# Low parts of split weights in the scan stage: an adding DMA onto a negated copy, in place of a GpSimd subtraction

## The chip, the cores and the metric

The kernel runs on one core of a Trainium2 chip. The metric is the time of one execution on the device in microseconds (us), the median of several runs.

## What is computed

One layer of a hybrid backbone: 512 latent tokens of width 1024, with 256 context tokens whose scan states start the latent scans. The part that the change touches is the input projection and the three branches that read it:

```
h    = modulated_norm(x, g_norm1, sh1, sc1)
proj = h @ w_in                      # 1024 x 7712, cut into z, xBC, dt, pool, gmlp, gates
xbc  = silu(dwconv(proj[xBC]))       # 5 taps
y    = ssd_scan(...)  both directions, 128-token chunks, states from the context
y_pool = box means of proj[pool];  y_gmlp = u * (ws @ layernorm(v))
x    = x + g1 * ((gates * branches) @ w_o)
x    = x + g2 * moe(...)             # top-1 group, top-2 experts, 16 experts
out  = rmsnorm(x)
```

All in float32.

## The kernel before

Each weight matrix is multiplied in three products of float32r (a rounded float32 that TensorE takes at full speed): rounded weights by rounded activations, rounded weights by the activations' remainder, and the weights' remainder by rounded activations. So every weight unit, a tile of 128 x 1024 float32 (512 KB), is loaded from HBM into a ring of four buffers (`raw`), and `split` makes two tiles of it: `hi`, which ScalarE copies and rounds (L87), and `lo = raw - hi` (L89), from rings of three buffers each. Which engine does the subtraction is set by `lo_eng`. It is VectorE (`V`) at the start and from the SSD norm on, and GpSimd (`G`) between: from the first pair of `x` channels in the scan loop to the end of the gMLP branch.

```
        S.activation(hi[:, :n], raw[:, :n], AF.Copy)
        with tc.issue_after(after.ins) if after else nullcontext():
            eng.tensor_tensor(lo[:, :n], raw[:, :n], hi[:, :n].bitcast(FT), op=OP.subtract)
```

That stretch, called the scan stage here, runs from about 60 to 415 us. In it 34 units go through GpSimd. The loop over four head groups does, for each group, four `xbc_tile` calls (one unit each: projection, then the convolution as one ScalarE and four VectorE operations `cv` on L968 and L970, a silu, transposes on TensorE), `ssd_decay` (the DMA `agb<-agd` on L1112, then ScalarE and VectorE operations on L1119 to L1133), in every second group a `z_block` (four units, a `tm_block`), and `ssd_group` (states on L1075 to L1085, outputs on L1094 to L1104). After the loop come the pooling mixer (VectorE sums on L1260 to L1280) and the gMLP branch (L1215 to L1237), with 12 units more.

The order of the instructions on each engine is made by a scheduler when the program is built. At run time each engine follows its own list in order and waits on semaphores. TensorE (PE) takes a unit's `hi` in the first products and its `lo` in the product of L105 (in `xbc_tile` and `cm_block`) or L1145 (in `tm_block`). SyncE (SP) issues the loads of `raw` and `agb` in one in-order queue, and a load into a `raw` buffer waits until the subtraction that last read the buffer is done. GpSimd (POOL) also issues some small DMAs, and late in the kernel the scatter `eod<-eo` of L445, an adding DMA of 512 KB to HBM.

Of the kernel before, what the change touches and what calls it, by code (L numbers as in the profile page):

```python
# [11 lines left out]
AF = mybir.ActivationFunctionType  # L12
OP = mybir.AluOpType
# [30 lines left out]
def backbone_kernel(ctx: ExitStack, tc: tile.TileContext, x, c, ctxt, c_ctx, w_mod, b_mod, g_norm1,  # L44
# [4 lines left out]
    V, S, G, T = nc.vector, nc.scalar, nc.gpsimd, nc.tensor  # L49
# [31 lines left out]
    def split(raw, n, after=None):  # L81
        nsplit[0] += 1
        eng = G if lo_eng[0] is None and nsplit[0] % 1000 == 3 else lo_eng[0] or V
        hp_, lp_ = more_hl if more_hl and nsplit[0] % 4 == 0 else (hip, lop)
        hi = hp_.tile([128, 1024], FR, tag="hi", name="hi")
        lo = lp_.tile([128, 1024], FR, tag="lo", name="lo")
        S.activation(hi[:, :n], raw[:, :n], AF.Copy)  # L87
        with tc.issue_after(after.ins) if after else nullcontext():
            eng.tensor_tensor(lo[:, :n], raw[:, :n], hi[:, :n].bitcast(FT), op=OP.subtract)  # L89
        return hi, lo  # L90

    def unit(ap, k, n):
        raw = rawp.tile([128, 1024], FT, tag="raw", name="raw")
        nc.sync.dma_start(raw[:, :k * n].rearrange("p (k n) -> p k n", k=k), ap)
        hi, lo = split(raw, k * n)
        return (hi[:, :k * n].rearrange("p (k n) -> p k n", k=k),
                lo[:, :k * n].rearrange("p (k n) -> p k n", k=k))
# [31 lines left out]
    def late_rows(stack, rd):  # L129

        ap_ = stack.enter_context(pool("lrow"))
        oner = ap_.tile([128, 4], FR)
        V.tensor_copy(oner, ones[:, 0:4])

        def block(b):
            a = ap_.tile([128, D], FT, tag="lacc", name="lacc")
            G.memset(a, 0.0)
            nc.sync.dma_start(a[0:1], dap(b_mod, (2 + b) * D, [[D, 1], [1, D]]))
            for k in range(KD):
                raw = rawp.tile([128, 1024], FT, tag="raw", name="raw")  # L140
                nc.sync.dma_start(raw, dap(w_mod, k * 128 * 6144 + (2 + b) * D, [[6144, 128], [1, D]]))
                V.scalar_tensor_tensor(a, raw, sc[:, k:k + 1], a, op0=OP.mult, op1=OP.add)  # L142
            hi, lo = split(a, D)
            r = ap_.tile([1, D], FT, name="lr", tag="lr")
            if b == 2:
                gn = rawp.tile([128, 1024], FT, tag="raw", name="gn2")[0:1]
                nc.sync.dma_start(gn, dap(g_norm2, 0, [[D, 1], [1, D]]))
            for h in range(2):
                cs = slice(h * 512, (h + 1) * 512)
                pr = ptmp([4, 512])  # L150
                T.matmul(pr, lhsT=oner, rhs=hi[:, cs], start=True, stop=False)
                T.matmul(pr, lhsT=oner, rhs=lo[:, cs], start=False, stop=True)
                if b == 2:
                    V.scalar_tensor_tensor(r[:, cs], pr[0:1], 1.0, gn[:, cs], op0=OP.add, op1=OP.mult)
                else:
                    S.activation(r[:, cs], pr[0:1], AF.Copy)
            nc.sync.dma_start(rd[b:b + 1], r)
        return block
# [189 lines left out]
    def moe(q):  # L348
# [29 lines left out]
        def munit(e, k, out_w, widx):  # L378
            rows = w2rows if out_w else w1rows
            if widx is None:  # L380
                n = nraw[0] % 31
                nraw[0] += 1
                raw = ring[n]
                if isinstance(raw, tuple):
                    raw = raw[0].tile([128, 1024], FT, tag=raw[1], name=raw[1])
                r0 = e * (DE if out_w else D) + k * 128
                nc.sync.dma_start(raw, rows[r0:r0 + 128])
            else:
                raw = rawp.tile([128, 1024], FT, tag="raw", name="raw")
                c0 = k + (KD if out_w else 0)  # L390
                G.indirect_dma_start(out=raw, out_offset=None, in_=rows,
                                     in_offset=bass.IndirectOffsetOnAxis(ap=widx[:, c0:c0 + 1], axis=0))
            return split(raw, 1024, chain[0] if widx is None and nraw[0] <= 4 else None)
# [992 lines left out]
```

## Time and profile before

| | us |
|---|---|
| median of 3 runs (1037.62 to 1039.67) | 1037.87 |
| the profiled execution's own time | 1038.74 |
| its span in the trace | 1036.9 |
| busy in the span: PE | 946.9 (91%) |
| busy: VectorE (DVE) | 820.9 (79%) |
| busy: ScalarE (ACT) | 596.9 (58%) |
| busy: GpSimd (POOL) | 189.7 (18%), of it 91.1 in the 34 subtractions of L89 |

The time of an execution is the span and 1.84 us around it. Busy shares are means over stages with different limits: PE is the fullest engine, and yet a stretch can be set by a chain of small steps on other engines. The chain of work that ended last is 64% PE and 22% DVE over the whole span.

### The profile page before, as it was taken

What the parts mean: (1) busy time and instruction counts of PE and PEld (TensorE: products, weight loads), DVE (VectorE), ACT (ScalarE), POOL (GpSimd) and SP (SyncE); (2) the same over time, 40 slices, a digit from 0 to 9 for tenths busy, and PEclk for the clock granted to TensorE, in tenths of its full rate; (3) what the DMA queues carried; (4) which work ended last, traced back from release to release, by engine and by line L of the source; (5) the groups of instructions that cost most, each with busy time, mean ns of one, the idle gap of its engine ahead of it and who ended that gap; (6) DMA issues with size and microseconds to landing.
All of it is one profiled execution on the core that took longest, in us unless ns stands there. A gap on an engine that the chain in (4) does not pass through costs nothing.

```text
span 1036.9 us, 13348 instructions
## 1 busy us (share of the span) xinstructions
PE 946.9 (91%) x4598; PEld 769.4 (74%) x4598; DVE 820.9 (79%) x1221; ACT 596.9 (58%) x884; POOL 189.7 (18%) x144
## 2 busy tenths in 40 slices
PE   3897989998898979999999999978999999999964
PEld 0486778886786857888888888867888888888842
DVE  6878976997878996677486434579999999999897
ACT  5665846667556333622332432445788888888843
POOL 2024313114222340000000010331111111111140
PEclk9998999999999989999999999988999999999987
DMA  8832361314223222276576558678999999999322
GB/s 271 280 91 60 119 201 41 116 47 143 61 61 86 64 65 71 82 244 215 172 217 210 162 166 288 257 245 318 326 355 362 361 375 372 375 361 364 107 73 82
DMA packets 100898, 203.92 MB, mean 197 GB/s; under 512 B 9998, under 2 KB 55290, under 8 KB 100827
## 3 DMA queue, kind: packets, MB, share of 16 engines
q1 hardware_dynamic: 95474, 194.19, 54.5%
q0 software_dynamic: 5136, 8.78, 3.6%
q8 instruction: 37, 0.61, 0.2%
q14 instruction: 35, 0.28, 0.1%
q10 hardware_dynamic: 216, 0.07, 0.0%
HBM read 197.25 MB, written 13.71 MB: 203 GB/s over the span
## 4 chain that ended last, share of the span: by engine, by line
PE 64%; DVE 22%; ACT 5%; DMA 4%; issue 3%; ACTq 0%; POOL 0%; SPq 0%; DVEq 0%; POOLq 0%
PE pacc L104 18%; PE pacc L103 18%; PE pacc L105 18%; DVE cv L970 5%; DVE lo L89 2%; PE ptmp L400 1%; DMA wraw<-in_w_mod_dram 1%; DVE w L1132 1%; DMA agb<-agd 1%; PE ptmp L1094 1%; PE ptmp L1096 1%; DVE agb L1126 1%; PE ptmp L423 1%; DVE r L1274 1%; DVE y L1103 1%
## 5 line engine op out<-in xcount | busy, mean ns | idle before, releaser
L87 ACT ACTIVATE hi<-raw 128x1024 fp32r<-128x1024 f32 (+1 forms) x199 | 209.0, 1057 | 168.0 <-PE pacc L104 75.9
L89 DVE TENSOR_TENSOR lo<-raw,hi 128x1024 fp32r<-128x1024 f32 (+1 forms) x165 | 203.6, 1254 | 58.8 <-ACT hi L87 51.7
L103 PE MATMUL pacc<-hTh,hi 128*128 128x512 f32 (+1 forms) x392 | 156.7, 401 | 4.9 <-ACT ytok L1168 3.5
L104 PE MATMUL pacc<-hTl,hi 128*128 128x512 f32 (+1 forms) x392 | 158.0, 403 | 0.0
L105 PE MATMUL pacc<-hTh,lo 128*128 128x512 f32 (+1 forms) x392 | 156.6, 400 | 0.0
L104 PE MATMUL pacc<-lo,xhl 128*128 128x512 f32 x384 | 151.5, 395 | 4.2 <-DVE lo L89 3.9
L103 PE MATMUL pacc<-hi,xhl 128*128 128x512 f32 x384 | 153.1, 402 | 0.0
L105 PE MATMUL pacc<-hi,xhl 128*128 128x512 f32 x384 | 150.5, 393 | 0.0
L89 POOL TENSOR_TENSOR lo<-raw,hi 128x1024 fp32r<-128x1024 f32 x34 | 91.1, 2684 | 197.6 <-ACT hi L87 187.8
L103 PEld LDWEIGHTS pacc<-hTh,hi 128*128 128x128 f32 (+1 forms) x392 | 74.0, 189 | 21.5 <-ACT ytok L1168 3.9
L104 PEld LDWEIGHTS pacc<-lo,xhl 128*128 128x128 f32 x384 | 72.9, 190 | 20.4 <-DVE lo L89 6.1
L970 DVE SCALAR_TENSOR_TENSOR cv<-xr,pcol,cv 128x770 f32<-128x770 f32 (+1 forms) x64 | 70.9, 1108 | 20.9 <-ACT cv L968 20.2
L105 PEld LDWEIGHTS pacc<-hTh,lo 128*128 128x128 f32 (+1 forms) x392 | 73.9, 189 | 16.2 <-issue 1.0
L104 PEld LDWEIGHTS pacc<-hTl,hi 128*128 128x128 f32 (+1 forms) x392 | 74.0, 189 | 16.0 <-issue 1.1
L105 PEld LDWEIGHTS pacc<-hi,xhl 128*128 128x128 f32 x384 | 72.5, 189 | 15.5
L103 PEld LDWEIGHTS pacc<-hi,xhl 128*128 128x128 f32 x384 | 72.9, 190 | 14.6
L142 DVE SCALAR_TENSOR_TENSOR lacc<-raw,sc,lacc 128x1024 f32<-128x1024 f32 x32 | 41.1, 1284 | 29.4 <-DMA raw<-in_w_mod_dram 29.0
L89 DVE TENSOR_TENSOR lo<-r,hi 128x1024 fp32r<-128x1024 f32 x42 | 50.1, 1219 | 4.7 <-PE pacc L104 3.0
L87 ACT ACTIVATE hi<-r 128x1024 fp32r<-128x1024 f32 x42 | 44.0, 1062 | 7.8 <-PE pacc L105 7.2
L480 POOL DMA_INDIRECT xg<-h2d,toki x16 | 19.2, 1201 | 156.8 <-PE ptmp L400 82.5
L1145 PE MATMUL pacc<-lo,hTh 128*128 128x512 f32 x96 | 38.6, 402 | 0.0
L1144 PE MATMUL pacc<-hi,hTh 128*128 128x512 f32 x96 | 38.2, 398 | 0.0
(410 smaller groups left out, 1894.8 us busy)
## 6 DMA issues: line engine op xcount, KB each, us to landing
raw<-in_w_e_in_dram SPq DMA_DIRECT2D x78, 512.0 KB
raw<-in_w_in_dram SPq DMA_DIRECT2D x60, 512.0 KB
raw<-in_w_e_out_dram SPq DMA_DIRECT2D x36, 512.0 KB
raw<-in_w_mod_dram SPq DMA_DIRECT2D x32, 512.0 KB
r<-in_w_e_in_dram SPq DMA_DIRECT2D x28, 512.0 KB
wraw<-in_w_mod_dram SPq DMA_DIRECT2D x16, 512.0 KB
agb<-agd SPq DMA_DIRECT2D x16, 512.0 KB
r<-in_w_e_out_dram SPq DMA_DIRECT2D x14, 512.0 KB
```

The source lines that it names most:

```text
L87: S.activation(hi[:, :n], raw[:, :n], AF.Copy)
L89: eng.tensor_tensor(lo[:, :n], raw[:, :n], hi[:, :n].bitcast(FT), op=OP.subtract)
L103: T.matmul(ps, lhsT=sh, rhs=mh, start=first, stop=False)
L104: T.matmul(ps, lhsT=sh, rhs=ml, start=False, stop=False)
L105: T.matmul(ps, lhsT=sl, rhs=mh, start=False, stop=last)
L142: V.scalar_tensor_tensor(a, raw, sc[:, k:k + 1], a, op0=OP.mult, op1=OP.add)
L400: T.transpose(pt[:, k], xgt[:, (h * 4 + k) * 128:(h * 4 + k + 1) * 128], ident)
L423: T.transpose(pt[:, k], hid[:, k * 128:(k + 1) * 128], ident)
L480: G.indirect_dma_start(out=dst, out_offset=None, in_=h2d[:, :], in_offset=bass.IndirectOffsetOnAxis(ap=idx, axis=0), bounds_check=L - 1, o ...
L970: V.scalar_tensor_tensor(oo, r[:, lo0 + j:lo0 + j + n], wcol(j), oo, op0=OP.mult, op1=OP.add)
L1144: T.matmul(pv[t], lhsT=a, rhs=wh[:, kk], start=k == 0, stop=False)
L1145: T.matmul(pv[t], lhsT=a, rhs=wl[:, kk], start=False, stop=False)
```

## The change

When the engine is GpSimd, ScalarE writes `lo = -round(raw)` with a second copy at scale -1, and GpSimd issues a DMA that adds `raw` onto `lo` in place. The subtraction on GpSimd is gone. Splits whose engine is VectorE are as they were. Behind L88 the line numbers of the changed kernel are four higher.

```diff
         S.activation(hi[:, :n], raw[:, :n], AF.Copy)
+        if eng is G:
+            S.activation(lo[:, :n], raw[:, :n], AF.Copy, scale=-1.0)
+            G.dma_start(lo[:, :n], raw[:, :n], accum_op=OP.add)
+            return hi, lo
         with tc.issue_after(after.ins) if after else nullcontext():
             eng.tensor_tensor(lo[:, :n], raw[:, :n], hi[:, :n].bitcast(FT), op=OP.subtract)
```

On GpSimd, in the first head group, the list was this (`agd<-ar` are small stores of the decay sums):

```order
L89 TENSOR_TENSOR lo<-raw,hi 128x1024 x3
L1026 DMA mx<-in_gmlp_ws_dram 128x4x128
L1037 IOTA mx 128x64
L1039 IOTA mx 128x8
L89 TENSOR_TENSOR lo<-raw,hi 128x1024
L942 DMA agd<-ar 4x4x128 x8
L89 TENSOR_TENSOR lo<-raw,hi 128x1024 x20
```

and is now this:

```order
L90 DMA lo<-raw 128x1024 x3
L1030 DMA mx<-in_gmlp_ws_dram 128x4x128
L1041 IOTA mx 128x64
L1043 IOTA mx 128x8
L90 DMA lo<-raw 128x1024
L946 DMA agd<-ar 4x4x128 x8
L90 DMA lo<-raw 128x1024 x20
```

Nothing moved there: each subtraction became the issue of a DMA at the same place. On ScalarE, at the second `z_block` (its results leave as `ytok`), the list was this:

```order
L87 ACTIVATE hi<-raw 128x1024
L1125 ACTIVATE w<-agb,nag 128x128 x4
L1131 ACTIVATE w<-cbu,dtt 128x128 x2
L1128 ACT_TABLE_LOAD
L1128 ACTIVATE agb<-agb 128x512
L1131 ACTIVATE w<-cbu,dtt 128x128 x2
L1125 ACTIVATE w<-agb,nag 128x128 x4
L1131 ACTIVATE w<-cbu,dtt 128x128
```

and is now this:

```order
L87 ACTIVATE hi<-raw 128x1024
L89 ACTIVATE lo<-raw 128x1024
L87 ACTIVATE hi<-raw 128x1024
L1129 ACTIVATE w<-agb,nag 128x128 x4
L1135 ACTIVATE w<-cbu,dtt 128x128 x2
L1132 ACT_TABLE_LOAD
L1132 ACTIVATE agb<-agb 128x512
L1135 ACTIVATE w<-cbu,dtt 128x128 x2
```

A `lo` stands behind its `hi`, and the next unit's `hi` ahead of the decay's operations; that unit's own `lo` comes only after the `z_block` has left. On SyncE, in the same group, the list was this:

```order
L94 DMA raw<-in_w_in_dram 128x2x512 x3
L1112 DMA agb<-agd 128x1024
L94 DMA raw<-in_w_in_dram 128x2x512
L1112 DMA agb<-agd 128x1024 x3
L94 DMA raw<-in_w_in_dram 128x8x128 x4
```

and is now this:

```order
L98 DMA raw<-in_w_in_dram 128x2x512 x3
L1116 DMA agb<-agd 128x1024 x2
L98 DMA raw<-in_w_in_dram 128x2x512
L1116 DMA agb<-agd 128x1024 x2
L98 DMA raw<-in_w_in_dram 128x8x128 x3
```

The second `agb` load now stands ahead of the weight load that it stood behind.

## Rows read from the trace of the kernel before

**Rows 1.** Windows (us, engines' busy us, PE's granted clock, DMA share): scan stage, later stretch.

```profile
60.00:415.00 355.00, 321.98 (x1647) 267.61 (x1646) 293.90 (x540) 203.54 (x373) 101.76 (x62) 0.97 0.30 87
500.00:600.00 100.00, 100.00 (x442) 81.94 (x441) 58.55 (x62) 32.10 (x44) 0.96 (x1) 1.00 0.59 185
```

**Rows 2.** Waits of PE in the scan stage: us, times, longest.

```profile
PE ptmp L1286 <- DVE o L1280: 7.4, 2, 6.0
PE ptmp L990 <- ACT cv L983: 6.6, 5, 2.6
PE ptmp L924 <- DVE inv L1046: 5.4, 1, 5.4
PE ptmp L1075 <- DVE h L1085: 5.2, 5, 1.7
PE pacc L103 <- ACT ytok L1168: 3.5, 2, 3.2
```

**Rows 3.** Timeline (start us, us): one subtraction on POOL, DVE beside it and later.

```profile
119.17 2.62 POOL L89 TENSOR_TENSOR lo<-raw,hi 128x1024 fp32r<-128x1024 f32 x1 [7.69 <-ACT hi L87]
...
119.45 2.89 DVE L1133 TENSOR_TENSOR w<-w,agb 128x512 f32<-128x512 f32 x1
...
132.43 0.69 DVE L1133 TENSOR_TENSOR w<-w,agb 128x512 f32<-128x512 f32 x1
```

**Rows 4.** Lines, DVE in the scan stage: busy us, mean ns, idle before.

```profile
L970 DVE SCALAR_TENSOR_TENSOR cv<-xr,pcol,cv 128x770 f32<-128x770 f32 x48 | 59.1, 1231 | 20.9 <-ACT cv L968 20.2
...
L1133 DVE TENSOR_TENSOR w<-w,agb 128x512 f32<-128x512 f32 x16 | 17.3, 1082 | 0.1
...
L1103 DVE TENSOR_TENSOR y<-y,xd 128x256 f32<-128x256 f32 x16 | 13.1, 817 | 0.0
```

**Rows 5.** The same lines by source: shortest, median, longest ns.

```profile
L970 DVE SCALAR_TENSOR_TENSOR cv<-xr,pcol,cv x64: 734/1013/3208, 75.8 to 310.0; 128x770 f32<-128x770 f32 x48, 128x512 f32<-128x512 f32 x16
...
L1103 DVE TENSOR_TENSOR y<-y,xd x16: 405/416/2620, 150.8 to 348.7; 128x256 f32<-128x256 f32 x16
```

**Rows 6.** Chain that ended last, in the scan stage: start us, us, what.

```profile
71.95 2.35 DVE dw L916
...
195.67 4.71 DMA agb<-agd
...
297.18 3.16 DVE cv L970
...
384.07 2.27 DVE rv L115
```

**Rows 7.** POOL's subtractions and scatters by source (ns; DMA us), timeline around a scatter.

```profile
L89 POOL TENSOR_TENSOR lo<-raw,hi x34: 2366/2565/3766, 69.3 to 383.8; 128x1024 fp32r<-128x1024 f32 x34
...
L445 POOL DMA_INDIRECT eod<-eo,toki x14: 1558/1577/2027, 741.5 to 976.8; - x14
...
DMA to landing us min/median/max: 6.2/8.9/9.5
...
760.22 1.67 POOL L445 DMA_INDIRECT eod<-eo,toki  x1 [4.60 <-ACT eo L454]
...
760.46 0.69 DVE L425 TENSOR_TENSOR xhl<-ptmp,xhl 128x512 fp32r<-128x512 f32 x1
```

**Rows 8.** DMA issues in the scan stage: KB, us to landing.

```profile
mx<-in_gmlp_ws_dram POOLq DMA_DIRECT2D x1, 256.0 KB, 3.2
```

**Rows 9.** Lines, ACT in the scan stage: busy us, mean ns, idle before.

```profile
L87 ACT ACTIVATE hi<-raw 128x1024 fp32r<-128x1024 f32 x38 | 40.1, 1056 | 45.8 <-issue 21.0 <-PE pacc L104 8.6 <-PE pacc L1146 6.2
```

**Rows 10.** Timeline: the first and the 17th subtraction, and PE's first use of each.

```profile
69.32 2.39 POOL L89 TENSOR_TENSOR lo<-raw,hi 128x1024 fp32r<-128x1024 f32 x1 [8.86 <-ACT hi L87]
...
75.61 0.39 PE L105 MATMUL pacc<-hTh,lo 128*128 128x512 f32 x1
...
233.65 2.40 POOL L89 TENSOR_TENSOR lo<-raw,hi 128x1024 fp32r<-128x1024 f32 x1 [17.37 <-ACT hi L87]
...
239.12 0.48 PE L1145 MATMUL pacc<-lo,hTh 128*128 128x512 f32 x1
```

## The prediction

> **What bounds the kernel now.** I read the windows first, to see how full each engine is in the stage that the change touches. From 60 to 415 us PE is busy 322.0 of 355 us and idle 33.0; DVE is busy 293.9 (83%), ACT 203.5 (57%), POOL 101.8, and the DMA engines 30% [rows 1]. In a later stretch, 500 to 600 us, PE is busy without a gap, so the stage has at most those 33 us of PE's idle time to give, and a little more: its granted clock is 0.97 of full speed on average, which is 0.03 x 355 = 10.6 us of full-speed work.
>
> Next the waits of PE. The four longest make 24.6 of the 33 us, and all stand behind DVE: three directly, and the one behind ACT's silu of L983 through the convolution steps `cv` of L970 that the silu waits for [rows 2]. So in this stage PE is held up by DVE, in places.
>
> Then DVE and POOL side by side in the timeline. While POOL subtracts for 2.62 us, DVE's L1133 takes 2.89 us; the same operation takes 0.69 us when POOL is idle [rows 3]. The reader is to see that DVE doesn't run slower there, it stands still: the longest cases are the usual time plus about 2.15 us, whatever the size of the operation (L1103: 0.42 and 2.62; L970: 1.01 and 3.21) [rows 5]. A subtraction takes 2.37 us at the shortest [rows 7], so one DVE operation waits for nearly all of it. The excess over the undisturbed time shows in the means: L970 48 x (1.231 - 1.013) = 10.5 us, L1103 16 x (0.817 - 0.416) = 6.4 [rows 4, 5], and L1133 16 x (1.082 - 0.69) = 6.3 [rows 3, 4]: 23 us in three groups. With 34 subtractions at 2.15 us each the bound is 73 us; the ones beside an idle DVE cost nothing. My estimate for the whole is 50 us.
>
> Last the chain that ended last. Stretched DVE operations are links in it from 71.95 to 384.07 us, some 25 of them [rows 6]. At about 1.7 us of excess on average (1.2 to 2.2) that is some 40 us of the chain.
>
> **The change, part by part.**
>
> *The subtraction goes.* With it go DVE's stalls, if issuing a DMA on POOL doesn't stall DVE too. The trace has such issues: while POOL issues the adding scatter of L445 for 1.67 us, DVE's L425 runs inside that time in its usual 0.69 us [rows 7]. So all of it goes. What that is worth on PE: from above, the 40 us of the chain, which PE's 33.0 us of idle time and 10.6 us of clock would just hold; from below nothing, if another wait is right behind each stall. Each of the four waits of rows 2 has stalls ahead of it that are as long or longer (ahead of L924 alone the chain holds three, from 71.95 us on), so in principle all 24.6 us go. PE's list is fixed, and where one wait is taken away PE runs sooner into the next product that isn't ready; I take four fifths, 20 us, and 3 us for the clock, which should rise where PE no longer pauses. Gain: 23 us.
>
> *ACT gets a second copy.* 34 x 1.06 us = 36 us by the row of `hi` [rows 9]. ACT goes from 203.5 to about 240 us, which in a stage of some 335 us is 71% instead of 57%. From below this costs nothing, since ACT is idle 150 us; from above all 36 us, if every copy stood in the chain. PE waits for ACT's silus 6.6 + 3.5 = 10.1 us now [rows 2]. Waits behind a queue grow about as busy over idle, from 57/43 to 71/29, so nearly double; half of what is there goes away with the stalls. I take 5 us.
>
> *The low part comes later.* Before, it was there 2.6 us after `hi`. Now it takes a copy of 1.06 us and then a DMA of 512 KB from SBUF to SBUF with an addition. The trace of before has no such DMA. From below, the plain 256 KB load that POOL issues lands after 3.2 us [rows 8]; from above, the adding scatter of 512 KB lands after up to 9.5 us, among full DMA queues, and after 6.2 us in the quickest case [rows 7]. With the DMA engines 30% busy here I take 6.2. So `lo` is 1.06 + 6.2 - 2.6 = 4.7 us later. What hides that is the ring of three: `lo` is made well ahead. The first subtraction ended at 71.71 us and PE took its result at 75.61, 3.9 us later; the 17th ended at 236.05 and was taken at 239.12, 3.1 us later [rows 10]. These are the two tightest of the 34; in the 32 others 6 to 23 us lie between. So PE waits 0.8 + 1.6 = 2.4 us. If a DMA took 9.5 us, seven units would be late, by some 15 us together. The Trainium skill, in "DMA: Bandwidth & Descriptors", section "Anatomy of one DMA — SWDGE (gpsimd) path", gives 2.0 us + bytes / 436 GB/s for a DMA issued there, an estimate of 3.2 us for 512 KB. By that no unit would be late and the sum would be 2.4 us better; the page's formula doesn't speak of additions, and the trace's adding DMA of this size never landed before 6.2 us, so I go by the row.
>
> *The raw buffer comes free later,* by the same 4.7 us, and SP's load into it is held up, with what stands behind it in SP's list. That are `agb` loads, one of which is 4.71 us of the chain [rows 6]. In the new list the second `agb` load of that group stands ahead of the weight load. DMA traffic grows by 34 x 0.5 MB, and an `agb` load can meet it. I take 1 us, between nothing and 5 us (all of that one link again).
>
> *POOL* issues for about 1.6 us [rows 7] where it subtracted for 2.6; nothing waits for POOL otherwise.
>
> Sum: -23 + 5 + 2.4 + 1 = -14.6 us. The profiled execution took 1038.74 us, so 1024.1; it stood 0.9 us above the median of the runs, so I put the changed kernel at **1023.5 us**.
>
> **The rivals.**
>
> *Nearly all of the chain's 40 us come back.* If PE's list, made for a DVE without stalls, then runs without pauses, the gain is PE's idle 33 us less 3 for late units: about 1009. For it speaks that all of DVE's stalls have one cause; against it that ACT is at 71%.
>
> *The gain goes into ACT.* ACT and DVE hand work to each other in this stage (DVE waits 20.2 us for L968 [rows 4]). If half of the new copies (18 of 36 us) stand in the chain, the gain of 23 us is gone: 1038.7 - 23 + 18 + 3.4 = 1037, no change that can be told (a measurement of this kernel tells from no change about 0.2%, 2 us). Against it: the chain's large links here are DVE's.
>
> *The low part is late in every unit of the runs of units.* In the two `z_block`s and behind the loop 20 units follow one another, each 24 products at 100 / 442 = 0.226 us [rows 1], 5.4 us of PE. With three buffers the split of a unit can begin when PE is done with the third unit before it, so it has 2 x 5.4 = 10.9 us; two copies leave 8.8 us for the DMA and ACT's queue. Beyond that point every three units lose the difference. At 9.5 us for the DMA and 4 us in ACT's queue it is 4.7 us x 20 / 3 = 31 us, and the kernel is slower: 1038.7 - 23 + 6 + 31 = 1053. Some of the new copies do stand far behind their `hi` in ACT's list, which speaks for it; against it, the DMA engines are 30% busy here, so 6.2 us is the nearer row.
>
> *The change doesn't do what it says:* DVE is stalled by something else at those places, or by the new DMA as well. Rows 3 and 7 speak against it. It would cost the ACT part and the lateness: 1038.7 + 8 = 1047.
>
> **How the numbers follow.** I give my forecast (8 to 24 us gained) 0.55, the large gain (24 to 36) 0.13, a small gain of 2 to 8 us 0.13, the gain lost within 2 us 0.07, late low parts 0.08 and no effect on the stalls 0.04. Faster by over 0.2% is the first three, 0.81; the same 0.07; slower 0.12. The range from 1006 to 1037 leaves out the slower cases, half of the unchanged and a little of the large gain. The likeliest case's own range is 1014 to 1030.
>
> **What would show it.** In the changed profile DVE's L970 at 128 x 770 should have a mean near 1.01 us, and no DVE operation in the stage its usual time plus 2 us. ACT should be busy about 36 us more, the scan stage should end near 400 us, and the work behind it should take what it took. The adding DMAs should land about 6 us after their issue, and PE should wait for them in two or three places, for a few us. I am wrong if PE waits for `lo` in the runs of units, if ACT takes DVE's place in the chain with its new copies, or if DVE's operations beside the new DMAs are still stretched.

## The result and the profile after

The changed kernel takes 1011.36 us (median of 4 runs, 1009.57 to 1014.56), the kernel before 1037.74 on the same chip: ratio 0.9748, 95% interval 0.9729 to 0.9768, 26.4 us faster. The profiled execution took 1009.57 us at a span of 1007.8.

Nearly all of the difference lies in the scan stage. Its end is marked by the first square of the SSD norm on ScalarE: 412.1 us before, 385.1 after, 27.0 us earlier; the end of the span comes 29.1 us earlier, as the work behind the mark takes 622.7 us and took 624.8. These are the windows of the stage cut at that mark (us, engines' busy us, PE's granted clock, DMA share), first of before, with the time ahead of the stage and three short stretches that are used below:

```profile
0.00:60.00 60.00, 39.24 (x176) 19.36 (x176) 43.60 (x78) 33.42 (x43) 6.25 (x20) 0.94 0.81 251
60.00:412.10 352.10, 319.08 (x1634) 265.20 (x1633) 292.46 (x538) 200.64 (x369) 101.76 (x62) 0.97 0.30 88
...
80.00:90.00 10.00, 5.92 (x38) 5.05 (x36) 10.00 (x27) 5.21 (x8) 2.48 (x4) 0.91 0.10 26
90.00:100.00 10.00, 8.63 (x45) 7.48 (x46) 8.71 (x19) 4.25 (x9) 4.13 (x8) 0.75 0.23 58
370.00:380.00 10.00, 5.88 (x13) 3.41 (x14) 10.00 (x26) 2.38 (x5) 3.54 (x3) 0.66 0.36 105
```

and of after, with the time ahead of the stage and two short stretches:

```profile
0.00:60.00 60.00, 41.66 (x185) 22.10 (x186) 44.55 (x80) 34.21 (x46) 6.67 (x20) 0.94 0.81 253
60.00:385.10 325.10, 310.59 (x1626) 260.57 (x1625) 236.42 (x536) 228.46 (x402) 39.93 (x61) 0.99 0.62 150
...
130.00:140.00 10.00, 7.32 (x40) 5.77 (x39) 4.88 (x15) 8.77 (x14) 2.57 (x3) 1.00 0.95 248
140.00:150.00 10.00, 10.00 (x47) 8.57 (x48) 6.72 (x14) 1.29 (x5) 0.00 (x0) 0.83 1.06 228
```

PE's idle time falls from 352.1 - 319.1 = 33.0 us to 325.1 - 310.6 = 14.5, which is 18.5 us. PE's busy time in the stage falls by 8.5 us. Of that the clock gives 5.4: PE is busy for 14.3 us at the lower of its two clock levels before and for 3.4 now, and half of such time is the price. Most of the other 3.1 us are products that the changed kernel has already run before 60 us (185 for 176, 2.4 us more of busy time). Together that is the 27.0. DVE is busy 56 us less, with 536 operations for 538.

What PE waits for now (us, times, longest), where [rows 2] stood:

```profile
PE pacc L109 <- DMA lo<-raw: 3.8, 2, 2.7
PE pc L109 <- DMA lo<-raw: 3.6, 2, 2.1
PE pacc L1149 <- DMA lo<-raw: 2.4, 2, 1.5
PE ptmp L928 <- DVE inv L1050: 2.0, 1, 2.0
PE pacc L107 <- ACT ytok L1172: 1.5, 1, 1.5
PE ptmp L1079 <- DVE h L1089: 0.8, 2, 0.6
```

The waits behind the convolution and the pooling sums are gone; 9.8 of the 14.5 us are waits for the new DMA, in six places. The operations of [rows 4] as lines (busy us, mean ns, idle before), then by source as in [rows 5] (shortest, median, longest ns):

```profile
L974 DVE SCALAR_TENSOR_TENSOR cv<-xr,pcol,cv 128x770 f32<-128x770 f32 x48 | 48.8, 1016 | 22.6 <-ACT cv L972 22.0
...
L1137 DVE TENSOR_TENSOR w<-w,agb 128x512 f32<-128x512 f32 x16 | 10.9, 684 | 0.1
```

```profile
L974 DVE SCALAR_TENSOR_TENSOR cv<-xr,pcol,cv x64: 744/1016/1023, 73.9 to 298.4; 128x770 f32<-128x770 f32 x48, 128x512 f32<-128x512 f32 x16
...
L1107 DVE TENSOR_TENSOR y<-y,xd x16: 411/418/425, 149.2 to 331.8; 128x256 f32<-128x256 f32 x16
...
L90 POOL DMA_DIRECT2D lo<-raw x34: 850/860/953, 69.5 to 360.3; - x34
...
DMA to landing us min/median/max: 4.5/5.0/10.3
```

The longest `cv` took 3208 ns before and takes 1023 now. GpSimd's issue of an adding DMA takes 0.86 us, and the DMA lands 5.0 us after the start of its issue (both are medians; the last line is that of L90). The timeline (start us, us) shows one unit on its way through ScalarE, then the issue and the first use of the next unit, and last an issue with DVE beside it, which is what [rows 3] showed for the subtraction:

```profile
101.18 1.06 ACT L87 ACTIVATE hi<-raw 128x1024 fp32r<-128x1024 f32 x1 [0.38 <-PE pacc L1150]
...
109.32 1.05 ACT L89 ACTIVATE lo<-raw 128x1024 fp32r<-128x1024 f32 x1
...
110.68 0.88 POOL L90 DMA_DIRECT2D lo<-raw  x1 [11.49 <-ACT lo L89]
...
115.83 0.50 PE L1149 MATMUL pacc<-lo,hTh 128*128 128x512 f32 x1 [1.46 <-DMA lo<-raw]
115.87 0.85 POOL L90 DMA_DIRECT2D lo<-raw  x1 [4.32 <-ACT w L1135]
...
123.87 0.39 PE L109 MATMUL pc<-hC,lo 128*128 128x256 f32 x1 [2.08 <-DMA lo<-raw]
...
156.88 0.86 POOL L90 DMA_DIRECT2D lo<-raw  x1 [16.95 <-ACT lo L89]
156.90 0.42 DVE L1107 TENSOR_TENSOR y<-y,xd 128x256 f32<-128x256 f32 x1
```

DVE's `y` takes its usual 0.42 us beside the issue. The unit's `hi` was ready at 102.24, but ScalarE came to its `lo` only at 109.32, with the scan's decay work and a silu between; PE then waited 1.46 us for the DMA. For the next unit it waited 2.08 us, and there the DMA itself was slow: it landed 7.95 us after its issue, just before 123.87. On ScalarE the 34 new copies are one line, as forecast:

```profile
L89 ACT ACTIVATE lo<-raw 128x1024 fp32r<-128x1024 f32 x34 | 36.1, 1062 | 12.1 <-PE pacc L1149 12.1
```

### The profile page after: what moved, and what is told of

Its sections match the earlier page's. It is cut to its first block, busy times and chain, and to the rows that moved or that the text cites. A ratio compares the mean times of both kernels' runs of the same rounds, so it can differ in the third digit from the quotient of the medians.

```text
span 1007.8 us, 13404 instructions
## 1 busy us (share of the span) xinstructions
PE 939.7 (93%) x4598; PEld 766.6 (76%) x4598; DVE 765.2 (76%) x1221; ACT 625.4 (62%) x918; POOL 129.6 (13%) x144
## 4 chain that ended last, share of the span: by engine, by line
PE 76%; issue 7%; DVE 7%; ACT 5%; DMA 4%; POOL 0%; ACTq 0%; SPq 0%; DVEq 0%; POOLq 0%
PE pacc L109 20%; PE pacc L108 20%; PE pacc L107 20%; DVE lo L93 2%; DMA lo<-raw 2%; PE ptmp L404 2%; PE ptmp L1098 1%; PE ptmp L1100 1%; ACT hi L87 1%; PE ptmp L1079 1%; PE pacc L1148 1%; PE pacc L1149 1%; PE pacc L1150 1%; PE ptmp L427 1%; PE ptmp L834 1%
## 5 line engine op out<-in xcount | busy, mean ns | idle before, releaser
L108 PE MATMUL pacc<-hTl,hi 128*128 128x512 f32 (+1 forms) x392 | 155.7, 398 | 0.0
L107 PEld LDWEIGHTS pacc<-hi,xhl 128*128 128x128 f32 x384 | 72.7, 189 | 14.3
L974 DVE SCALAR_TENSOR_TENSOR cv<-xr,pcol,cv 128x770 f32<-128x770 f32 (+1 forms) x64 | 60.8, 950 | 23.4 <-ACT cv L972 22.7
L90 POOL DMA_DIRECT2D lo<-raw x34 | 29.4, 865 | 236.2 <-ACT lo L89 154.5
L89 ACT ACTIVATE lo<-raw 128x1024 fp32r<-128x1024 f32 x34 | 36.1, 1062 | 12.1 <-PE pacc L1149 12.1
L1149 PE MATMUL pacc<-lo,hTh 128*128 128x512 f32 x96 | 38.3, 399 | 2.4 <-DMA lo<-raw 2.4
```

Of the source, the lines that this page charges most:

```text
L89: S.activation(lo[:, :n], raw[:, :n], AF.Copy, scale=-1.0)
L90: G.dma_start(lo[:, :n], raw[:, :n], accum_op=OP.add)
L107: T.matmul(ps, lhsT=sh, rhs=mh, start=first, stop=False)
L108: T.matmul(ps, lhsT=sh, rhs=ml, start=False, stop=False)
L974: V.scalar_tensor_tensor(oo, r[:, lo0 + j:lo0 + j + n], wcol(j), oo, op0=OP.mult, op1=OP.add)
L1149: T.matmul(pv[t], lhsT=a, rhs=wl[:, kk], start=False, stop=False)
```

## The experiments

**Theory A**, the stalls: the time was lost because GpSimd's subtraction holds VectorE, and comes back because issuing a DMA does not. **The rival**, the order: the stretched operations are harmless, and the gain comes from the new instruction lists (what stands where on ScalarE and SyncE, less work in GpSimd's queue). "Stalled" below is my own sum over the trace of 60 to 470 us: each DVE operation's time less the shortest of its form in any run, where that is over 0.15 us. It is 58.8 us before, in 34 operations, and 0.2 after.

**1. The stalls put back, all else equal.** After the DMA's issue GpSimd subtracts `hi` from itself into a scratch tile that nobody reads. The lists of the other four engines stay as in the changed kernel, row for row.

```diff
             G.dma_start(lo[:, :n], raw[:, :n], accum_op=OP.add)
+            for cs in (slice(0, 512), slice(512, 1024)):
+                G.tensor_tensor(junk, hi[:, cs].bitcast(FT), hi[:, cs].bitcast(FT), op=OP.subtract)
             return hi, lo
```

> The changed kernel, and for each of the 34 units GpSimd also subtracts hi from hi into a scratch tile that nobody reads (two operations of 128 x 512, about 1.3 us each, as soon as hi is there, where the old subtraction stood). The lists of ScalarE, VectorE, TensorE and SyncE are the same as in the changed kernel, row for row. Theory A (the 26 us came from VectorE's stalls beside a GpSimd operation that reads SBUF): the stalls are back, so the time is 1035 to 1046 us, and VectorE's 128 x 770 convolution step has a mean of 1.2 us again. Rival B (the gain came from the new order of the lists or from buffers that come free sooner): 1010 to 1014 us.

Measured: 1035.87 us, ratio to before 0.9979 (0.9958 to 1.0001). The lines:

```profile
L977 DVE SCALAR_TENSOR_TENSOR cv<-xr,pcol,cv 128x770 f32<-128x770 f32 x48 | 56.2, 1170 | 22.2 <-ACT cv L975 21.5
...
L93 POOL TENSOR_TENSOR junk<-hi 128x512 bf16<-128x512 f32 x68 | 90.0, 1324 | 120.7 <-ACT hi L88 118.1
```

PE's waits, and then the window of the stage:

```profile
PE ptmp L997 <- ACT cv L990: 4.7, 4, 3.2
PE ptmp L1082 <- DVE h L1092: 4.2, 4, 3.3
PE ptmp L931 <- DVE inv L1053: 4.1, 1, 4.1
PE ptmp L1293 <- DVE o L1287: 4.0, 2, 3.4
```

```profile
60.00:412.30 352.30, 324.46 (x1635) 268.66 (x1634) 270.36 (x538) 230.58 (x404) 127.33 (x130) 0.96 0.57 139
```

The same four places as in [rows 2] are back. The only wait for the added work itself is one of 3.3 us, by ScalarE's `hi` for its buffer (before, such waits for the subtraction were 17.6 us). PE's waits for `lo` are 8.2 us, for 9.8 in the changed kernel, so it isn't GpSimd's longer list that makes `lo` late. VectorE was stalled 35.7 us in 51 operations, and 24 of the 26 us are lost again. About half of the loss is idle time of PE (27.8 us for 14.5), and most of the rest is the clock: PE is busy for 25.8 us at the lower level, for 3.4 in the changed kernel, in six stretches, four behind waits for VectorE's work and two behind waits for `lo`. Theory A stands; the order as the cause falls.

**2. GpSimd busy without two inputs.** First with three fills of the scratch tile per unit (`G.memset(junk, 0.0)`):

> The changed kernel, and for each of the 34 units GpSimd also fills a scratch tile three times (it writes SBUF and reads nothing); the other engines' lists are the same as in the changed kernel. Theory A with the narrower claim that a GpSimd operation must read SBUF to hold VectorE up: no change, 1009 to 1014 us. Rival (any GpSimd work that touches SBUF holds VectorE up): 34 x three fills of about 0.3 to 0.5 us, half or more of it as stalls, 1018 to 1030 us.

Measured: 1015.25 us, ratio 0.9791 (0.9751 to 0.9831), `cv` at its usual 1016 ns. But nothing makes a fill wait for its unit, and most of the 102 ran in GpSimd's idle time before 60 us. The time lies between the two forecasts, so this shows little. Then with copies of `hi`, which do wait:

```diff
-                G.tensor_tensor(junk, hi[:, cs].bitcast(FT), hi[:, cs].bitcast(FT), op=OP.subtract)
+                G.tensor_scalar(junk, hi[:, cs].bitcast(FT), 1.0, None, op0=OP.mult)
```

> The changed kernel, and for each of the 34 units GpSimd also copies hi into a scratch tile (two operations of 128 x 512 with one SBUF input in place of two); the other engines' lists are the same as in the changed kernel. Theory A as stated (any GpSimd operation that reads SBUF holds VectorE for its length): the loss goes with the length of the operation; at 0.5 to 1.3 us each 1020 to 1036 us. Narrower rival (GpSimd must read two tensors to hold VectorE): 1010 to 1016.

Measured: 1025.39 us, ratio 0.9878 (0.986 to 0.9895). GpSimd is busier than with the subtractions (115.7 against 90.0 us), VectorE stalled less, 14.9 us in 37 operations, and 15 us are lost against the changed kernel on the same chip (1010.48, experiment 5). One input is enough to hold VectorE, so the narrower rival falls. But not all of the 15 us need be stalls: ScalarE's `hi` also waits 10.2 us, four times, until the copies have read its buffer. The timeline of this kernel, then that of the subtractions at the same place (start us, us):

```profile
105.54 5.40 POOL L93 TENSOR_SCALAR junk<-hi 128x512 bf16<-128x512 f32 x3
...
107.92 1.39 DVE L977 SCALAR_TENSOR_TENSOR cv<-xr,pcol,cv 128x770 f32<-128x770 f32 x1
109.23 1.50 DVE L1133 SCALAR_TENSOR_TENSOR agb<-agb,ag,w 128x128 f32<-128x128 f32 x4
```

```profile
124.29 3.07 POOL L93 TENSOR_TENSOR junk<-hi 128x512 bf16<-128x512 f32 x2 [1.82 <-ACT hi L88]
...
125.26 2.77 DVE L1133 SCALAR_TENSOR_TENSOR agb<-agb,ag,w 128x128 f32<-128x128 f32 x4
```

Four L1133 take 1.50 us beside the copies (one of them is 0.38 us late) and 2.77 beside the subtractions (two are held, 0.79 and 0.86 us).

**3. The subtraction on VectorE.** No GpSimd, no second copy, no DMA (`eng = V` where it was `G`).

> The old subtraction, but on VectorE for all units: no GpSimd operation beside VectorE, no adding DMA, no second copy on ScalarE; VectorE gets 34 x 1.22 = 41 us of work. Theory A: the stalls (some 50 us of VectorE's time) go and 41 us of work come, spread evenly instead of in holds of 2.15 us, so a part of the gain is there: 1018 to 1032 us. Rival E (VectorE has room for 41 us, the adding DMA was not needed): 1008 to 1014. Rival B (order): no forecast, but 1035 or more would speak against A.

Measured: 1032.05 us, ratio 0.9946 (0.9926 to 0.9966).

```profile
L91 DVE TENSOR_TENSOR lo<-raw,hi 128x1024 fp32r<-128x1024 f32 x39 | 47.4, 1219 | 37.2 <-ACT hi L87 33.1 <-PE ptmp L1234 4.2
```

Without stalls, and yet 21 us slower than the changed kernel, at the upper edge of Theory A's forecast; rival E falls: 34 x 1.22 = 41 us on VectorE cost more than 36 us on ScalarE and the DMA together.

**4. What ScalarE's time is worth.** First the negated copy made twice (the line stands twice), which also makes `lo` later:

> The changed kernel with the negated copy made twice on ScalarE, so that ScalarE has another 36 us of work in the scan stage. Theory A with ScalarE's copies priced at 5 us for the first 34: the second 34 cost 5 to 12 us, 1016 to 1023 us. Rival C (ScalarE is off the path, its copies are free): 1010 to 1014. Rival D (ScalarE now sets the end of the stage): 25 us or more, 1036 and above.

Measured: 1024.53 us, ratio 0.9870 (0.983 to 0.9911), 13 us above the changed kernel and just above my step's forecast. Then two copies of halves of `hi` to the scratch tile behind the issue, so that `lo` isn't made later by them directly:

> The changed kernel, and behind each adding DMA's issue ScalarE copies both halves of hi to a scratch tile that nobody reads: 68 copies of 128x512, an estimated 45 us of ScalarE (a copy of 128x1024 takes 1.06 us) that don't make the low part itself later by construction. My step that prices 36 us of ScalarE at 5 us says 1015 to 1018 us. Rival (ScalarE's time in this stage is worth a third of itself, as the kernel with two negated copies suggests): 1022 to 1027 us. If only the low part's lateness counts and not ScalarE's time: within 2 us of 1011.

Measured: 1025.07 us, ratio 0.9883 (0.9851 to 0.9915). The line, and PE's waits:

```profile
L93 ACT ACTIVATE junk<-hi 128x512 bf16<-128x512 f32 x68 | 42.6, 626 | 0.5
```

```profile
PE pacc L1152 <- DMA lo<-raw: 10.0, 4, 3.7
PE ptmp L1082 <- ACT hc L1084: 7.5, 2, 4.6
```

42.6 us of ScalarE cost 14 us, about a third. The waits for `lo` are no longer than in the changed kernel (10.4 us with a short one, against 9.8): new are 7.5 us behind ScalarE's `hc`, and PE's busy time in the whole span is 946.3 us against 939.7, at a lower clock. My step's price, 5 for 36, is too low for a further copy; the rival's third fits both kernels. It is no clean price: the scheduler's lists for ScalarE and VectorE differ elsewhere too.

**5. The negated copy first.** Copy and DMA are written ahead of `hi`'s copy.

```diff
+        if eng is G:
+            S.activation(lo[:, :n], raw[:, :n], AF.Copy, scale=-1.0)
+            G.dma_start(lo[:, :n], raw[:, :n], accum_op=OP.add)
         S.activation(hi[:, :n], raw[:, :n], AF.Copy)
         if eng is G:
-            S.activation(lo[:, :n], raw[:, :n], AF.Copy, scale=-1.0)
-            G.dma_start(lo[:, :n], raw[:, :n], accum_op=OP.add)
             return hi, lo
```

> The changed kernel with the negated copy and the adding DMA written ahead of the copy that makes hi, so that lo starts one ScalarE copy (1.06 us) sooner. Theory A with late low parts as the largest wait left (TensorE waits 9.8 us for the adding DMA, in six places): 3 to 7 us faster than the changed kernel, 1004 to 1009. Rival (those waits are replaced by the next ones, or hi is now late): 1009 to 1015.

Measured: **1001.11 us**, ratio 0.9643 (0.9626 to 0.9659), and beside it on the same chip the changed kernel once more:

> The changed kernel once more, so that the runs beside it have it on the same chip: 1009 to 1015 us.

Measured: 1010.48 us, ratio 0.9726 (0.971 to 0.9743). So this order gives another 9.4 us, more than the 3 to 7 that I expected, and this version beats both kernels. Two waits of PE, the longest and the one for `lo`, the window of the stage, and its landings:

```profile
PE pacc L108 <- ACT ytok L1173: 2.4, 1, 2.4
...
PE pc L110 <- DMA lo<-raw: 0.8, 1, 0.8
```

```profile
60.00:375.80 315.80, 309.37 (x1633) 261.56 (x1631) 237.20 (x538) 226.78 (x402) 40.11 (x62) 0.99 0.64 155
```

```profile
DMA to landing us min/median/max: 4.5/5.2/7.6
```

PE's idle time is 6.4 us, and it waits 0.8 us for `lo`, not 9.8, with as many copies on ScalarE and a DMA that is no quicker in the median (5.2 us; the trace tells 18 of its 34 landings). The scheduler's lists differ elsewhere too, so the 9.4 us are those of the order as a whole.

**6. The low part much later.** A second adding DMA per unit adds zeros onto `lo`, in pieces of 512 bytes (`G.dma_start(lo..., z0..., accum_op=OP.add)`).

> The changed kernel with a second adding DMA per unit behind the first, which adds zeros, so that lo comes about 5 us later and the DMA engines move 17.8 MB more; ScalarE, VectorE and TensorE have the same work. Theory A with the ring of three as cover: units with less than 5 us in hand are late, in the runs of units above all, 10 to 25 us in all, 1021 to 1036. Rival (the cover is ample): 1010 to 1016. Rival (as my third rival had it, every unit of the runs late): 1045 and above.

Measured: 1094.57 us, ratio 1.0529 (1.0505 to 1.0554), far above the 1021 to 1036 of Theory A and in the range of the last rival. PE's waits, and the landings of the first and the second DMA:

```profile
PE pacc L1152 <- DMA lo<-z: 27.2, 7, 12.0
PE pacc L112 <- DMA lo<-z: 25.5, 9, 5.2
```

```profile
DMA to landing us min/median/max: 4.6/7.8/8.8
...
DMA to landing us min/median/max: 6.6/7.1/16.3
```

The second issue stands in GpSimd's list and waits there for the first to land, 185 us in all, and the next unit's first DMA stands behind it. `lo` is then some 15 us behind its copy (7.8 + 7.1) where the prediction's third rival put the point at 8.8. So that rival's mechanism can set the time, here with the queue in GpSimd's list added to it; in the changed kernel the DMA stays below its point but for two landings (9.0 and 10.3 us), neither of which PE waits for.

**7. Where the gain is made.** The change in the scan loop's units alone, and in the 12 units behind the loop alone.

> The change in the scan loop's 22 units only; the 12 units behind the loop (pooling and gMLP) keep the subtraction on GpSimd. Theory: the gain is made where the stalls go, and adds up stage by stage. The outputs of the fourth head group came 16.9 us earlier in the changed kernel, so about 17 us of the 27 belong to the loop: 1018 to 1024 us. Rival: the loop's gain is only lent, and comes back only if the tail is free too: above 1029 us here, and near nothing for the tail alone.

> The reverse: the 22 units of the loop keep the subtraction, the 12 behind it use the adding DMA. Theory of gains that add up: the rest of the gain, some 10 us, so 1025 to 1031 us, and the two partial gains sum to 24 to 30 us. Rival (one stage decides alone): 1036 us or more here.

Measured: 1031.06 us, ratio 0.9934 (0.9914 to 0.9953), for the loop, and 1021.18, ratio 0.9851 (0.9819 to 0.9883), for the tail: 7.1 and 17.0 us, together 24.1 of 26.4. They add up, but the split is the reverse of what I expected, and neither time lies in its forecast. The loop's lies in the range of the rival that calls its gain lent; but by that rival the tail alone should have gained next to nothing. By source, the loop kernel's subtractions:

```profile
L94 POOL TENSOR_TENSOR lo<-raw,hi x12: 2347/2574/3607, 275.9 to 378.3; 128x1024 fp32r<-128x1024 f32 x12
```

Units written behind the loop are split from 276 us on, while the fourth head group still runs. The third group's outputs came as early as in the changed kernel (289 to 276 us); after that 12 subtractions stalled VectorE 23.5 us, more than the 21.8 us of before in that part, and 6 us went again. The dearest place stands behind the loop:

```profile
360.00:370.00 10.00, 4.97 (x19) 3.49 (x18) 10.00 (x24) 2.43 (x5) 4.34 (x6) 0.88 0.19 52
370.00:380.00 10.00, 10.00 (x33) 7.02 (x33) 10.00 (x27) 4.28 (x7) 3.46 (x4) 0.78 0.18 52
```

In these windows of the loop kernel VectorE is full, PE idles half of 10 us, and the clock is down to 0.78 in the 10 us behind; with the tail changed PE is busy without a gap from 360 to 380 us at clock 1.00.

**8. The negated copy on VectorE**, in the version of 5 (`V.tensor_scalar_mul(lo, raw, -1.0)`).

> Negated copy and adding DMA ahead of hi's copy, but the negated copy is made by VectorE and not by ScalarE: ScalarE loses 36 us, VectorE gets 34 scalings of 128x1024 with one input, an estimated 23 to 41 us (half a convolution step's 1.01 us at 770 columns scaled up, to a full one). If ScalarE's 36 us cost about 12 us and VectorE's as much per us, the two nearly cancel: 997 to 1006 us. Rival (VectorE is the engine that holds PE up, so its time costs more than ScalarE's): 1007 to 1016 us.

Measured: 1021.85 us, ratio 0.9855 (0.9822 to 0.9888), 20.7 us slower than with ScalarE's copy, above even the rival.

```profile
L88 DVE TENSOR_SCALAR lo<-raw 128x1024 fp32r<-128x1024 f32 x34 | 23.5, 695 | 20.4 <-PE pc L110 14.8 <-PE pacc L110 4.8 <-PE ptmp L110 0.6
```

23.5 us more on VectorE and 36 less on ScalarE: in this stage a microsecond of VectorE is far dearer. The lists changed too, so 20.7 is no clean price.

## Why the prediction was right, and where it was off

The direction and the mechanism were right, and the range held the time. The sum did not: it gave 1023.5 us for 1011.36, about half of the gain, and the time lies outside the likeliest case's own range, 1014 to 1030, in the case that had 0.13. The step that was mis-sized most is the gain, "20 us, and 3 us for the clock"; costs that were also set too low, by 4 us, hide a part of that.

**What bounds the stage.** Right: PE was held by VectorE, and VectorE by GpSimd. No operation has its usual time plus 2 us any more (the longest excess is 0.2), and experiment 1 shows that the stalls, by themselves, are worth nearly the whole net gain.

**The gain.** Forecast 23 us; by the ledger above 35.4 in the stage, 30.0 of idle time and 5.4 of clock. Of the 33.0 us of idle time all but 3.0 are gone; the rest of the 14.5 now are waits for `lo` (9.8) and for ScalarE (1.7). The four longest waits, 24.6 us, of which I took four fifths, fell to 2.8, so 21.8 came back, close to my 20. The 8.4 us of other waits I left out. Of these 4.2 stood behind VectorE, the two longest here, and all of them went too; 4.1 stood behind ScalarE, and the 1.7 left there are counted below.

```profile
PE ptmp L1096 <- DVE h L1085: 1.5, 1, 1.5
PE ptmp L1094 <- DVE h L1085: 1.3, 1, 1.3
```

I feared that PE would run into the next product that isn't ready; apart from `lo`, which I had priced by itself, that took 2.8 us and not 4.9. Some 3 us more were gained by products that now run before 60 us, which the prediction doesn't have.

**The clock.** In before's 80 to 90 us PE is busy 5.9 of 10 us, and the next 10 us run at 0.75 on average, part at the lower of the two levels, 1.2 GHz; 370 to 380 has 5.9 and 0.66. Four such places make nearly all of the 10.6 us that the prediction counted, but PE is idle for a part of them, and they lengthen its work by only 7.1 us. Three followed waits behind VectorE (directly or by its `cv`), and the fourth, from 250 us on, a wait of 3.2 us for ScalarE's `ytok`. So waits and clock weren't two terms with shares of their own: in both kernels each low stretch begins in a wait or just behind one. The reverse doesn't hold: with the change in the tail alone (experiment 7) PE waits 3.4 us for the same `ytok`, and the clock stays at 1.00 from 250 to 270 us. The changed kernel has one such place left (130 to 150 us), behind waits for the new DMA.

**ScalarE, 5 us, and the late low part, 2.4 us.** Together 7.4 forecast and 11.5 seen (9.8 + 1.7), but split otherwise. The copies took the 36.1 us forecast, and PE's direct waits for ScalarE fell from 10.1 to 1.7; what the first 34 copies cost beside that no run separates. The DMA was quicker than I took it (5.0 us for 6.2, issue 0.86 for 1.6). Of the two units named as late the first was not, and the 17th by 0.94 us for 1.6; the other five waits are at units that I had given 6 us and more. What was missing in "4.7 us later" is ScalarE's queue: the list ahead of the prediction shows a `lo` far behind its `hi`, and I put that into a rival, not into the sum. The DMA has its share, though its median was shorter than I took it: in two of the six waits (2.1 and 1.5 us) it landed after 7.95 and 8.6 us, and at 5.0 us neither wait would have been. In experiment 5, with the copy written first, all but 0.8 us of these waits are gone. The Trainium skill, in "DMA: Bandwidth & Descriptors", section "Anatomy of one DMA — SWDGE (gpsimd) path", gives 2.0 us + bytes / 436 GB/s, an estimate of 3.2 us; the quickest of the 34 took 4.5, so row and rule lay on either side of the 5.0.

**The `agb` loads, 1 us.** No wait of PE ends at them; no run separates their effect.

**The rivals.** "Nearly all of the chain's 40 us come back", put at 1009 with 0.13, is what happened, with 9.8 us of late low parts where it had 3. "The gain goes into ACT" fell. The low part late everywhere needed experiment 6; its sign, a wait for `lo` in a run of units, came for only 2.4 of the 9.8 us (L1149, in the `z_block`s). "Doesn't do what it says" fell with the issue at 156.88 us.

## What to carry to other kernels

Where a VectorE operation shows a fixed excess beside a GpSimd operation, count all of the waits behind VectorE as its price, the short ones and the clock lost behind them included. Work moved to an engine with idle time is also paid for by its place in that engine's list: put what a DMA still has to follow first. Hand GpSimd the issue of a DMA rather than an elementwise operation that reads SBUF while VectorE is what the others wait for.

## What the runs showed of the hardware

How long VectorE is held depends on GpSimd's operation, not on its own: about 2.15 us by a subtraction of 128x1024 (2.37 us at the shortest), about 0.85 by one of 128x512 (1.03), and only 0.4, never over 0.9, by a one-input copy of 128x512 that takes 1.48 us or more. VectorE goes on 0.1 to 0.2 us before the recorded end of a subtraction, and mostly about 1.0 us before that of a copy. The Trainium skill, in "SBUF — State Buffer", section "🔬 SBUF: two separate sides", calls the port pair of the two engines an exclusive lock, held for the whole instruction. The subtractions agree but for their last 0.2 us; the copy doesn't, it lets VectorE go after less than a third.

An adding DMA of 512 KB within SBUF landed after 5.0 us in the median (4.5 to 10.3), with the engines' DMA share at 0.62 in the stage. A second one onto the same tile in pieces of 512 bytes brought the share to 0.87 and the first one's landing to 7.8 us.
